# Gathered down rows of block 0 at the head of the scheduler's list in a hybrid mLSTM, attention and PEER layer

## The chip, the cores and the metric

The kernel runs on one core of a Trainium2 chip. The metric is the device time of one execution in microseconds (us): 3559.62 us before the change, the median of 3 runs (3559.3 to 3559.77). Lower is better. The engines are called PE (TensorE, matrix products), DVE (VectorE), ACT (ScalarE), POOL (GpSimd, which here only issues gathers) and SP (SyncE, which issues all other transfers).

## What is computed

One decoder layer on 1024 tokens of width 1024, in float32. The part that matters here, cut from the reference:

```python
proj = rmsnorm(x) @ w_in                     # queries, keys, values, gates
att_b = sliding_window_attention(...) @ w_branch_attn
ml_b = (mlstm_chunkwise(...) normed, gated) @ w_branch_mlstm
x = x + (sigmoid(gate_a) * att_b + sigmoid(gate_m) * ml_b) @ w_out
xb = rmsnorm(x)                              # PEER, per block of 128 tokens:
q = xb @ w_query
s = q against 2 x 128 sub keys, 8 heads      # scores
idx, gate = top 16 of the 16 x 16 sums of the two top 16, softmax
u = expert_down[idx]                         # 8 x 16 rows of 16384 for each token
act = gelu(sum over d of xb * u)
x = x + sum over k of gate * act * expert_up[idx]
```

## The kernel before, in words

The 1024 tokens are 8 blocks of 128. The **front** (`front`, L304) does the mixers, the residual and the PEER queries and scores for four groups of two blocks, one group after the other: groups 0 to 3 are blocks (0, 1), (2, 3), (4, 5) and (6, 7). Its weights come from HBM in tiles of 0.5 MB (`wpart`, L207), four of which are in flight (WB = 4); where the products are split for precision, ACT makes the high part `whi` (L214) and DVE the residual `wlo` (L215), and PE multiplies three times (L231 to L233). A weight tile serves 4 chunks of the contraction, for two blocks.

Within a group the order is: query, key and value projections, and the mLSTM's gate projections (`wif`); attention; the mLSTM; the gates with the branch projections (L229 on `attT` and `hmT`); the next group's normed input (`normed`); the output projection (L612, on `mixT`) with the addition of the residual (L614, `x2`); the query projection of PEER (L627, on `xbT`); and the scores (L640), which go to HBM and come back by block (L667, `sc<-sc_d`).

`topk` (L647, on DVE) finds the experts of a block. It is emitted for the group before, ahead of a group's front, with its priority put behind by LATER (`later`, L856), so that it fills gaps. For blocks 1 to 5, which are treated **densely**, `spread` (L712) writes the gates into a dense token by expert matrix: DVE makes one-hot operands `oi` and `oj` (L727, L730), PE multiplies them (L735), ACT copies (L736), SP stores (L738). The front calls it piece by piece (`fill`, L871) among the gates, the output and the query projection. Blocks 0, 6 and 7 are **sparse**: their expert rows are gathered.

After the front comes the dense part (`dense`): all experts in turn against blocks 1 to 5, PE bound, with the gathers and products of the sparse blocks spread through it, except one: block 0's rows of `expert_down`. These are gathered and multiplied in the front (`down`, L747, called at L884): 128 gathers on POOL (L743, `g<-down,idx`, 128 rows of 4 KB each) and 128 **products** on DVE (L756, a multiplication with `xb` summed over the row, which also reads out its accumulator into `act`). The pool `gather` (L98) has two tiles `g`; a gather waits until the product two before it has released its tile. The gathers need block 0's `idx`, which exists about 500 us into the run.

Each product is tied to an anchor: `pace` takes 128 evenly spaced ones of the marked matmuls of the front, from 0.4 to 0.95 of them, and `after` (L151) adds an order without a semaphore: the scheduler may place product i only after its anchor has been placed. Where it is placed from then on is up to priority: the scheduler builds each engine's list by taking, of the instructions that are ready in its own time, the one with the highest priority, and priority falls with the place in the program. `down` stands behind the whole front there. On the chip each engine then runs its list in order, and waits on semaphores only for data and buffers.

Of the kernel before, what the change touches and what calls it, by code (L numbers as in the profile page):

```python
# [88 lines left out]
def build(nc, tc, a, out, dbg=None):  # L89
# [8 lines left out]
    gp = pool("gather", 2)  # L98
# [52 lines left out]
    def after(ins, name):  # L151
        if name is not None:
            tc.add_manual_dep(ins.ins, name, NOSYNC, reason="pace")
# [587 lines left out]
    def fetch(p, table, idx, s):  # L741
        t = p.tile([P, D], F32, name="g")
        G.indirect_dma_start(out=t, out_offset=None, in_=a[table],  # L743
                             in_offset=bass.IndirectOffsetOnAxis(ap=idx[:, s:s + 1], axis=0))
        return t

    def down(r, b, pace, p):  # L747
        act = bp.tile([P, P], F32, name="act", bufs=1)
        xb = bp.tile([P, D], F32, name="xb", bufs=1)
        SY.dma_start(xb, xb_d[b])  # L750
        gain = p.tile([P, D], F32, name="g")
        SY.dma_start(gain, a["gain2"].to_broadcast([P, D]))
        V.tensor_tensor(xb, xb, gain, ALU.mult)
        for s in range(P):
            t = fetch(p, "down", r["idx"], s)
            ins = V.tensor_tensor_reduce(out=t, in0=t, in1=xb, scale=1.0, scalar=0.0, op0=ALU.mult,  # L756
                                         op1=ALU.add, accum_out=act[:, s:s + 1])
            after(ins, next(pace, None))
        coef = bp.tile([P, P], F32, name="coef")
        A.activation(coef, act, AF.Gelu)  # L760
        V.tensor_tensor(coef, coef, r["gate"].rearrange("p h k -> p (h k)"), ALU.mult)
        r["coef"] = coef
# [101 lines left out]
    res = {}  # L864
# [16 lines left out]
    names = anchors["front"]  # L881
    names = names[int(PACE0 * len(names)):int(PACE1 * len(names))]
    pace = iter([names[i * len(names) // P] for i in range(P)])
    down(res[0], 0, pace, gp)  # L884
    inner.close()
    gd = dense()
    names = anchors["dense"]
    pace = iter([names[int((PD0 + i * (PD1 - PD0) / (5 * P)) * len(names))] for i in range(5 * P)])
# [18 lines left out]
```

## Time and profile before

| | us |
|---|---|
| median of 3 runs | 3559.62 |
| the profiled execution, its time | 3545.12 |
| its span, first to last instruction | 3543.4 |
| PE busy | 3378.6 |
| DVE busy | 2743.1 |
| ACT busy | 1363.0 |
| POOL busy | 985.7 |

The profile is one execution on the chip. The front fills about the first half of the span, the dense part the rest. Busy shares are means over both. The views used below are: the page; the busy time of each engine in a window of the span; groups of instructions by line; waits, each put down to what ended it last; the chain of waits, which follows the work that ended last back in time; and the timeline. Times in them count from the start of the span.

### The profile page before, as it was taken

The numbers are of one execution on the slowest core, as the hardware profiler recorded it, in microseconds if no ns is written. First come the engines' busy times: TensorE is split into PE (matmuls) and PEld (weight loads), VectorE is DVE, ScalarE is ACT, GpSimd is POOL, SyncE is SP. The second block draws the span as 40 slices with busy tenths as digits, with TensorE's granted clock in tenths as the row PEclk, the third lists the DMA queues.
The fourth block names the chain that finished last, engine by engine and source line by source line (L and its number), as shares of the span: only waits on it lengthen the run. The fifth ranks groups of instructions, "written<-read, shape, count | busy, mean of one in ns | idle before, by whom it ended". The sixth has DMA issues, their size and how long they took to land.

```text
span 3543.4 us, 55473 instructions
## 1 busy us (share of the span) xinstructions
PE 3378.6 (95%) x20579; PEld 3044.3 (86%) x20579; DVE 2743.1 (77%) x6406; ACT 1363.0 (38%) x2730; POOL 985.7 (28%) x772
## 2 busy tenths in 40 slices
PE   7999999999998789989799999999999999999999
PEld 7898988888887678887688898999989999898998
DVE  5332689739898468988598988888888888889985
ACT  6652567338574346635322222222222222222221
POOL 0000000110001221110004654545455455545542
PEclk9999999999999888999899999999999999999999
DMA  4344434874378874686727988889888888888884
GB/s 149 108 143 166 164 115 145 256 261 141 117 212 252 274 247 150 206 244 174 252 101 276 329 307 321 321 284 329 285 315 305 294 321 299 312 308 302 325 288 160
DMA packets 386670, 846.66 MB, mean 239 GB/s; under 512 B 189280, under 2 KB 195168, under 8 KB 382304
## 3 DMA queue, kind: packets, MB, share of 16 engines
q1 hardware_dynamic: 275808, 440.42, 37.7%
q0 software_dynamic: 110592, 402.70, 32.5%
q8 instruction: 162, 2.65, 0.3%
q14 instruction: 108, 0.88, 0.1%
HBM read 780.11 MB, written 62.91 MB: 238 GB/s over the span
## 4 chain that ended last, share of the span: by engine, by line
PE 66%; DVE 13%; issue 8%; DMA 7%; POOL 3%; ACT 3%; SPq 0%; POOLq 0%; DVEq 0%; ACTq 0%
PE ph L809 19%; PE pj L229 8%; PE po L830 6%; PE po L833 6%; PE po L834 6%; PE pj L231 4%; PE pj L233 4%; PE pj L232 4%; DMA g<-down,idx 3%; POOL g L743 3%; DVE oi L727 2%; PE at L735 2%; DMA w<-wmain 1%; DVE g L756 1%; DMA g<-up,idx 1%
## 5 line engine op out<-in xcount | busy, mean ns | idle before, releaser
L743 POOL DMA_INDIRECT g<-down,idx x384 | 480.2, 1250 | 1769.3 <-DVE act L756 879.2
L743 POOL DMA_INDIRECT g<-up,idx x384 | 505.3, 1316 | 732.8 <-DVE acc L770 373.9
L756 DVE CUSTOM_DVE_ANT_0 g<-g,xb 128x1024 f32<-128x1024 f32 x384 | 462.6, 1219 | 167.2 <-DMA g<-down,idx 166.6
L770 DVE SCALAR_TENSOR_TENSOR acc<-g,coef,acc 128x1024 f32<-128x1024 f32 x384 | 491.7, 1281 | 46.8 <-DMA g<-up,idx 36.8
L830 PE MATMUL po<-hu,ah 128*128 128x512 f32 x1280 | 499.2, 390 | 2.3 <-DVE y L836 2.3
L809 PE MATMUL ph<-xbh,hd 128*128 128x320 f32 x2048 | 470.6, 311 | 31.7 <-ACT hd L797 22.8
L833 PE MATMUL po<-lu,ah 128*128 128x512 f32 x1280 | 498.5, 389 | 0.0
L834 PE MATMUL po<-hu,al 128*128 128x512 f32 x1280 | 498.1, 389 | 0.0
L809 PE MATMUL ph<-xbh,ld 128*128 128x320 f32 x2048 | 470.5, 311 | 5.3 <-DVE ld L798 5.3
L809 PE MATMUL ph<-xbl,hd 128*128 128x320 f32 x2048 | 469.9, 311 | 0.0
L797 ACT CAST hu<-rawu 128x1024 fp32r<-128x1024 f32 x128 | 131.5, 1051 | 738.9 <-PE po L834 557.0
L809 PEld LDWEIGHTS ph<-xbh,hd 128*128 128x128 f32 x2048 | 346.6, 189 | 35.3 <-ACT hd L797 23.2
L215 DVE TENSOR_TENSOR wlo<-w,whi 128x1024 fp32r<-128x1024 f32 x200 | 243.3, 1218 | 142.1 <-ACT whi L214 142.0
L809 PEld LDWEIGHTS ph<-xbh,ld 128*128 128x128 f32 x2048 | 345.1, 189 | 7.0 <-DVE ld L798 6.7
L809 PEld LDWEIGHTS ph<-xbl,hd 128*128 128x128 f32 x2048 | 345.6, 189 | 0.0
L214 ACT CAST whi<-w 128x1024 fp32r<-128x1024 f32 x200 | 209.3, 1047 | 235.9 <-DMA w<-wmain 100.1
L836 DVE TENSOR_TENSOR y<-po,y 128x512 f32<-128x512 f32 x320 | 218.2, 685 | 89.0 <-PE po L834 88.5
L830 PEld LDWEIGHTS po<-hu,ah 128*128 128x128 f32 x1280 | 240.3, 188 | 53.9 <-DVE y L836 4.7
L834 PEld LDWEIGHTS po<-hu,al 128*128 128x128 f32 x1280 | 240.3, 188 | 50.5 <-DVE al L820 0.3
L833 PEld LDWEIGHTS po<-lu,ah 128*128 128x128 f32 x1280 | 240.3, 188 | 48.5
L232 PE MATMUL pj<-wlo,hT 128*128 128x256 f32 x832 | 244.9, 295 | 23.9 <-DVE wlo L215 23.9
L231 PE MATMUL pj<-whi,hT 128*128 128x256 f32 x832 | 245.9, 296 | 1.1 <-ACT whi L214 1.1
(266 smaller groups left out, 6670.2 us busy)
## 6 DMA issues: line engine op xcount, KB each, us to landing
w<-wmain SPq DMA_DIRECT2D x328, 512.0 KB
rawd<-downT SPq DMA_DIRECT2D x128, 512.0 KB
rawu<-up SPq DMA_DIRECT2D x128, 512.0 KB
gate_d<-stage SPq DMA_DIRECT2D x40, 1024.0 KB
g<-gate_d SPq DMA_DIRECT2D x32, 1280.0 KB
x<-x SPq DMA_DIRECT2D x16, 512.0 KB
sc_d<-sc SPq DMA_DIRECT2D x16, 512.0 KB
sc<-sc_d SPq DMA_DIRECT2D x32, 256.0 KB
```

The costliest lines, as they stand in the source:

```text
L215: V.tensor_tensor(lo, t, hi.bitcast(F32), ALU.subtract)
L229: ins = T.matmul(ps, lh(c), rh(c), start=first, stop=last)
L231: T.matmul(ps, lh(c), rh(c), start=first, stop=False)
L232: T.matmul(ps, lh(c), rl(c), start=False, stop=False)
L743: G.indirect_dma_start(out=t, out_offset=None, in_=a[table], in_offset=bass.IndirectOffsetOnAxis(ap=idx[:, s:s + 1], axis=0))
L756: ins = V.tensor_tensor_reduce(out=t, in0=t, in1=xb, scale=1.0, scalar=0.0, op0=ALU.mult, op1=ALU.add, accum_out=act[:, s:s + 1])
L770: ins = V.scalar_tensor_tensor(acc, t, g, acc, ALU.mult, ALU.add)
L809: ins = T.matmul(ps[:, u, 0:W], w[:, c, :], x[:, c, u * W:u * W + W], start=first, stop=last)
L830: first = T.matmul(o, ah[:, tok], uh[:, cols], start=(e == 0), stop=False)
L833: T.matmul(o, ah[:, tok], ul[:, cols], start=False, stop=False)
L834: ins = T.matmul(o, al[:, tok], uh[:, cols], start=False, stop=(e == EG - 1))
L836: V.tensor_tensor(y[:, k, cols], o, y[:, k, cols], ALU.add)
```

## The change

The call of `down` for block 0 is put into the scheduler's `high_priority` block. Everything that it issues (the load of `xb`, the load of `gain2`, the product of both, the 128 gathers, the 128 products, the gelu and its gating) then has a higher priority than everything else. The anchors stay. The number and kind of instructions are the same.

```diff
--- before.py
+++ after.py
@@ -881,7 +881,8 @@
     names = anchors["front"]
     names = names[int(PACE0 * len(names)):int(PACE1 * len(names))]
     pace = iter([names[i * len(names) // P] for i in range(P)])
-    down(res[0], 0, pace, gp)
+    with tc.high_priority():
+        down(res[0], 0, pace, gp)
     inner.close()
     gd = dense()
     names = anchors["dense"]
```

What it moves, at three places. In the names the number behind the underscore is that of the tile; `g_17479` is the tile of product 1, and each further product's number is 3 higher.

On DVE, in the query and key projection of group 2 (`qkms` is the sum of squares of its heads, `sc`, `tv`, `ti`, `bps`, `bv` and `cand` belong to the top-k of block 2). Before:

```order
L215 TENSOR_TENSOR wlo_8860<-w_8857,whi_8859 128x1024
L318 TENSOR_REDUCE qkms_7939<-sq_8262 128x2
L655 MAX_INDEX bps_7500<-bv_7471,cand_7497 128x8
L657 MATCH_REPLACE cand_7497<-bv_7471,cand_7497 128x136 x2
L659 MAX bv_7471<-cand_7497 128x8
L318 TENSOR_REDUCE qkms_7939<-sq_8267 128x2
```

And now:

```order
L215 TENSOR_TENSOR wlo_8860<-w_8857,whi_8859 128x1024
L756 ISA g_17569,act_17473<-g_17569,xb_17474 128x1024
L756 ISA act_17473 128x1
L318 TENSOR_REDUCE qkms_7939<-sq_8262 128x2
L659 MAX tv_7473<-sc_7475 128x8
L661 MAX_INDEX ti_7474<-tv_7473,sc_7475 128x8
L215 TENSOR_TENSOR wlo_8894<-w_8891,whi_8893 128x1024
L756 ISA g_17572,act_17473<-g_17572,xb_17474 128x1024
L756 ISA act_17473 128x1
L318 TENSOR_REDUCE qkms_7939<-sq_8267 128x2
```

Products 31 and 32 now stand here, and the top-k, which had got to its candidates, is at its first maxima still.

On DVE, behind group 2's last addition of `x2`, where the first three weight residuals of group 3 (`wlo_12751` and two more) stand. Before, the end of a row of 14 products, of which `g_17701` is product 75:

```order
L756 ISA g_17698,act_17473<-g_17698,xb_17474 128x1024
L756 ISA act_17473 128x1
L756 ISA g_17701,act_17473<-g_17701,xb_17474 128x1024
L756 ISA act_17473 128x1
L215 TENSOR_TENSOR wlo_12751<-w_12748,whi_12750 128x1024
L756 ISA g_17704,act_17473<-g_17704,xb_17474 128x1024
L756 ISA act_17473 128x1
L215 TENSOR_TENSOR wlo_12781<-w_12778,whi_12780 128x1024
L756 ISA g_17707,act_17473<-g_17707,xb_17474 128x1024
L756 ISA act_17473 128x1
L215 TENSOR_TENSOR wlo_12811<-w_12808,whi_12810 128x1024
```

And now, the end of a row of 5 products, with `g_17722` product 82:

```order
L756 ISA g_17716,act_17473<-g_17716,xb_17474 128x1024
L756 ISA act_17473 128x1
L756 ISA g_17719,act_17473<-g_17719,xb_17474 128x1024
L756 ISA act_17473 128x1
L756 ISA g_17722,act_17473<-g_17722,xb_17474 128x1024
L756 ISA act_17473 128x1
L215 TENSOR_TENSOR wlo_12751<-w_12748,whi_12750 128x1024
L215 TENSOR_TENSOR wlo_12781<-w_12778,whi_12780 128x1024
L215 TENSOR_TENSOR wlo_12811<-w_12808,whi_12810 128x1024
L756 ISA g_17725,act_17473<-g_17725,xb_17474 128x1024
```

Five products are left ahead of the three residuals and none between them; the others of that row stand in group 2 now.

On PE, at the end of group 2's gates (`hmT`) and the start of its output projection (`mixT`); L735 are the spread's products, of block 3, L716 and L269 transposes. Before:

```order
L229 MATMUL pj<-hmT,w 128x256 x4
L735 MATMUL at<-oj,oi 128x128 x4
L229 MATMUL pj<-hmT,w 128x256 x4
L735 MATMUL at<-oj,oi 128x128 x4
L229 MATMUL pj<-hmT,w 128x256 x4
L735 MATMUL at<-oj,oi 128x128 x4
L229 MATMUL pj<-hmT,w 128x256 x8
```

And now:

```order
L229 MATMUL pj<-hmT,w 128x256 x32
L229 MATMUL pj<-w,mixT 128x256 x16
L716 MATMUL tp<-identr,ef 128x128
L269 MATMUL tp<-identr,scr 128x128 x4
L229 MATMUL pj<-w,mixT 128x256 x4
L716 MATMUL tp<-identr,ef 128x128
L716 MATMUL tp<-identr,dgate 128x128
L229 MATMUL pj<-w,mixT 128x256 x2
L269 MATMUL tp<-identr,scr 128x128 x4
L229 MATMUL pj<-w,mixT 128x256
L735 MATMUL at<-oj,oi 128x128 x3
```

The spread's products of block 3 have left the gates, and begin in the output projection, behind the transposes of block 3's experts (L716).

## Rows read from the trace of the kernel before

**Rows 1.** Page, part 1: busy us (share of the span) and instructions of each engine.

```profile
PE 3378.6 (95%) x20579; PEld 3044.3 (86%) x20579; DVE 2743.1 (77%) x6406; ACT 1363.0 (38%) x2730; POOL 985.7 (28%) x772
```

**Rows 2.** Windows: busy us (instructions) of each engine, granted clock, DMA share, GB/s.

```profile
336.00:410.00 74.00, 71.75 (x482) 67.28 (x480) 26.15 (x70) 29.38 (x57) 0.00 (x0) 0.94 0.60 201
742.00:815.00 73.00, 70.52 (x483) 65.68 (x482) 35.08 (x90) 29.05 (x56) 8.26 (x8) 0.97 0.80 271
797.00:947.00 150.00, 149.26 (x1114) 128.97 (x1112) 138.49 (x555) 100.51 (x255) 4.31 (x3) 0.93 0.41 142
947.00:1191.00 244.00, 220.91 (x1411) 200.28 (x1410) 208.11 (x769) 136.00 (x332) 30.62 (x31) 0.95 0.76 222
1191.00:1299.00 108.00, 79.80 (x483) 73.27 (x481) 51.18 (x85) 30.49 (x57) 32.23 (x27) 0.83 0.81 274
...
1540.00:1600.00 60.00, 51.33 (x299) 45.82 (x299) 48.56 (x159) 14.46 (x31) 11.14 (x10) 0.94 0.84 266
```

**Rows 3.** Chain of waits, 1191 to 1299 us: shares of that stretch by line.

```profile
by line: issue 61.8%; POOL g L743 21.9%; DMA g<-down,idx 6.5%; PE pj L232 3.7%; PE pj L233 3.4%; PE pj L231 3.1%; DVE wlo L215 1.0%; POOLq L743 0.3%; DVE ti L655 0.3%; DVE tv L653 0.3%; DVE g L756 0.2%; DVE act L756 0.1%; DVEq L756 0.0%
```

**Rows 4.** Timeline of DVE: start us, us, what; in brackets idle before and releaser.

```profile
1199.47 1.23 DVE L756 CUSTOM_DVE_ANT_0 g<-g,xb 128x1024 f32<-128x1024 f32 x1 [5.78 <-DMA g<-down,idx]
...
1207.45 1.23 DVE L756 CUSTOM_DVE_ANT_0 g<-g,xb 128x1024 f32<-128x1024 f32 x1 [5.17 <-DMA g<-down,idx]
```

**Rows 5.** Windows for L756 alone: DVE busy us (records, two for a product).

```profile
742.00:815.00 73.00, 9.84 (x16) 0.97 0.80 271
797.00:947.00 150.00, 3.12 (x6) 0.93 0.41 142
947.00:1191.00 244.00, 38.00 (x62) 0.95 0.76 222
1191.00:1299.00 108.00, 33.24 (x54) 0.83 0.81 274
```

**Rows 6.** Waits of PE, 1191 to 1299 us: us in total, times, longest us.

```profile
PE pj L232 <- DVE wlo L215: 23.0, 4, 10.5
```

**Rows 7.** Chain of waits, 620 to 700 us: start us, us, what.

```profile
651.21 8.77 DMA g<-down,idx
...
664.10 0.12 PE pj L231
```

**Rows 8.** Page, part 5: busy us, mean ns of one, then idle before.

```profile
L756 DVE CUSTOM_DVE_ANT_0 g<-g,xb 128x1024 f32<-128x1024 f32 x384 | 462.6, 1219 | 167.2 <-DMA g<-down,idx 166.6
```

**Rows 9.** Waits of DVE, 947 to 1191 us.

```profile
DVE g L756 <- DMA g<-down,idx: 24.2, 13, 4.6
```

**Rows 10.** Waits of PE, 947 to 1191 us.

```profile
PE at L735 <- DVE oj L730: 12.8, 7, 4.2
PE at L735 <- DVE oi L727: 5.0, 1, 5.0
```

**Rows 11.** Groups by line, PE, 742 to 815 us: busy us, mean ns, idle before.

```profile
L229 PE MATMUL pj<-xbT,w 128*128 128x256 f32 x128 | 28.4, 385 | 0.0
```

**Rows 12.** Chain of waits, 1500 to 1700 us.

```profile
1548.54 7.24 issue
1556.01 7.78 DMA g<-down,idx
```

**Rows 13.** Groups by line, 960 to 1010 us.

```profile
L727 DVE TENSOR_SCALAR oi<-iota,cols 128x128 f32<-128x128 f32 x47 | 14.8, 338 | 0.3 <-ACT cols L717 0.3
...
L730 DVE TENSOR_SCALAR oj<-iota,cols 128x128 f32<-128x128 f32 x34 | 9.3, 277 | 0.0
```

**Rows 14.** Groups by line, 1066 to 1180 us.

```profile
L727 DVE TENSOR_SCALAR oi<-iota,cols 128x128 f32<-128x128 f32 x118 | 37.9, 355 | 2.0 <-PE at L735 2.0
...
L730 DVE TENSOR_SCALAR oj<-iota,cols 128x128 f32<-128x128 f32 x87 | 24.9, 286 | 0.0
...
L743 POOL DMA_INDIRECT g<-down,idx x24 | 23.2, 966 | 94.9 <-DVE act L756 50.9 <-DVE oi L727 43.0 <-DVE hTlow L277 1.1
```

**Rows 15.** Waits of SyncE's DMA queue, 797 to 947 us.

```profile
SPq L667 <- DVE ti L661: 16.5, 3, 15.5
```

## Prediction

> **What bounds the kernel now.** I read the page's busy shares first [rows 1]: TensorE (PE) is busy for 95% of the span, so work taken off another engine pays only where PE waits for it. The next view is therefore the busy time by stage [rows 2]. One stage comes back after each group of the front: from the query projection (L627) of one group, over its scores, to the end of the query, key and gate projections of the next. It is the same PE work each time, 482 or 483 matmul records, yet it took 74 us after group 0, 73 us after group 1 and 108 us after group 2. PE was busy in these for 71.75, 70.52 and 79.80 us, so the third has 28 us in which PE stood still; and its granted clock, which has the two levels 2.4 and 1.2 GHz, averaged 0.83 where the others had 0.94 and 0.97, so PE also spent more time on the same matmuls.
>
> What it waited for is in the chain of waits of that stage [rows 3]: "issue" 61.8%, the issue of gathers on GpSimd (POOL) 21.9%, gathers landing 6.5%, and hardly any PE. VectorE's (DVE) timeline shows why [rows 4]: one product of block 0 (L756) after another, with 5.78 and 5.17 us idle until a gather landed. The gather pool has two tiles, so a gather starts when the product two before it is done, and a run of products goes at the pace of gathers: 27 products (54 records, two each) in 108 us, 4 us each [rows 5]. In VectorE's order the weight residuals (wlo, L215) of group 3 stand behind 14 such products in a row, and PE waits 23.0 us for wlo in this stage [rows 6]. The same stage held 8 products after group 1 [rows 5] and none after group 0. So this stage is bound by a run of gathers, not by PE.
>
> The stretch before it (797 to 1191 us, group 2 itself) is another matter: VectorE was busy there for 138.49 of 150 and 208.11 of 244 us [rows 2], with 3 and 31 products [rows 5]. Most of the products due in the first of these windows came in the second or in the lump behind it, after top-k and spread work that stood ahead of them.
>
> **The change, part by part.** No instruction is added or taken away; block 0's gathers, products, gain load and gain product only move. The order shows where: of the 128 products, 1 to 3 come forward a little, 4 to 28 stay where they were, 29 to 76 come forward from the lump into group 2, most of the rest stay within some thirty places, and 115 to 121 come forward in group 3. GpSimd's order is the same list of gathers. SyncE's differs in where score reloads and spread stores stand among weight loads; the gain load goes to the front of its list, which costs one 0.5 MB transfer at the start and nothing on the path. From about 1680 us of before on, the orders of PE, VectorE and ScalarE are the same again, so the dense part shifts as a whole. I sum against the profiled execution (3545.12 us, span 3543.4); the median of the timed runs, 3559.62, is 14.5 us above it, and I carry the sum over unchanged.
>
> A. Around 650 us. In before, product 3 waited for a gather that could start only after product 1, which stood behind a block of spread work: 8.77 us of the chain [rows 7]. Products 1 and 2 now stand ahead of most of that spread work, so gather 3 has landed by the time product 3 is due. They also push 2 x 1.22 us [rows 8] into a stretch full of spread work. Between 8.77 - 2.44 = 6 us saved and 2 us lost; I take 4 saved, nearer the first, since the wait was on the chain.
>
> B. 797 us to the last addition of group 2's x2 (L614). By the order, 48 products stand ahead of that addition where 31 did: 17 more, 17 x 1.22 = 20.7 us of VectorE time, in a stretch that VectorE already bounds. What goes is its waiting for gathers, 24.2 us [rows 9]: 48 products over the 394 us of the two windows have 8 us each, twice the pace of 4 us. The difference is 3.5 us saved. But the spread work now comes in one bunch late in the group, with little PE work left to mix with; the price if PE and VectorE hand it to each other one by one is bounded by what PE lost to spread operands here, 12.8 + 5.0 = 18 us [rows 10]. I take 0, between 6 saved (every wait gone and two products' time hidden) and 18 lost, nearer to the difference, since both engines have the same work in sum.
>
> C. The 108 us stage. Now 5 products instead of 14 stand in a row ahead of group 3's first wlo: 5 x 4 = 20 us of gather pace, started when the x2 addition is done, against 28.4 us of query projection on PE [rows 11]; they are hidden. About 13 products fall in the stage, between the 8 of group 1 (73 us) and the 27 of before (108 us). On a line between these it would be 73 + 5 x 35/19 = 82 us; but at 4 us each 13 products need 52 us, less than PE's 73, so I take 75: 33 saved. The bounds are the 73 of group 1 and the 82 of the line, 35 and 26 saved. Part of this is clock: the matmuls that took 79.80 us of PE time here took 70.52 us after group 1.
>
> D. Group 3. Products 115 to 121 leave the lump at 1540 us, where the chain shows 7.24 us of issue and 7.78 us of a gather landing [rows 12] and PE was busy for 51.33 of 60 us [rows 2]. At most the 8.7 us of PE's gap and a little clock, 12 saved; at worst those 7 products delay spread work that PE waits for by 7 x 1.22 = 8.5 us, less the gap they leave, 5 lost. I take 5 saved: VectorE does the same work before the group's end either way.
>
> Sum: -4 + 0 - 33 - 5 = -42 us, 3503 in the profiled execution's terms, **3518 us** in the runs'. All good ends together are -6 - 6 - 35 - 12 = -59, all bad ends together +2 + 18 - 26 + 5 = -1.
>
> One thing speaks against moving gathers among spread work. The rows: the spread operands took 338 and 277 ns (oi, oj) in a stretch with one gather [rows 13] and 355 and 286 ns in one with 24 [rows 14]; 118 x 17 + 87 x 9 ns = 2.8 us, or 0.12 us per gather, 2 us for the 17 gathers that now fall there, inside B's bounds. The Trainium skill (SBUF — State Buffer, section Who interferes with whom) has VectorE and GpSimd share a port pair that the first to start holds for its whole instruction, and names tensor_scalar, which the spread operands are, among those that can take it. By that rule each of the 17 gathers could hold VectorE for its whole issue, and the sum would be some 16 us poorer; the trace's 0.12 us says that it hardly does.
>
> **The rivals.** (1) B goes wrong by its bound: spread products, bunched behind the moved products, hand PE and VectorE their operands one by one. For it: the bunch stands in the order; against it: x2's output projection is now mixed into it matmul by matmul. -42 + 18 = -24, 3536 us. (2) Each gather holds VectorE for its issue, 0.97 us [rows 14], 17 times in the bound stretch: -42 + 16 = -26, 3534 us. The row of 0.12 us speaks against it. (3) Nothing to be measured: the gather waits only move. Where pairs of products stand closer than 8 us the wait comes back, all 24.2 us of B's saving is lost (+18 by B's own bound), C gives its poorer 26, and A and D come out at +2 and 0: -6, 3554 us. For it: a few pairs in the order stand close together; against it: gathers landed in time wherever products were 8 us apart. (4) Slower: weight loads behind score reloads on SyncE. Top-k gives way to the products, so its score tiles come free later, and a reload (L667) at the head of SyncE's queue holds back the weights behind it. The longest such wait in before was 15.5 us [rows 15], most of which the weight tiles ahead of PE covered: four of them, each good for 24 matmuls (4 chunks, 2 blocks, 3 products) of 0.12 us [rows 7], 11.5 us. If all 16 reloads of groups 2 and 3 waited so long, PE would lose 16 x 4 = 64 us: -42 + 64 = +22, 3582 us; it is slower from the eleventh such wait on, and measurably so from the thirteenth. Against it: the reloads now stand further apart among the weights. (5) That the change does nothing can be ruled out by the order.
>
> **How the numbers follow.** The forecast, 3518, has a chance of 0.61; its own bounds are 3503 to 3538. Rival 1 has 0.18, rival 2 0.05, rival 3 0.09, rival 4 0.07. A measurement of this kernel tells about 0.2%, 7 us, from no change: below 3552.5 is faster. Forecast and rivals 1 and 2 make faster 0.84; rival 3 gives same 0.09, rival 4 slower 0.07. The range runs from 3503 to 3553: it leaves out rival 4, most of rival 3 and a little below C's and D's good ends, less than 2 in 10.
>
> **What would show it.** In the profile after: the stage from group 2's query projection to group 3's projections at some 75 us with a granted clock above 0.9 and PE's wait for wlo a few us (C); VectorE's waits for gathers ahead of it near zero, and group 2's query projection starting at 1185 to 1190 us (A, B); no lump at the end of group 3 (D). If that projection starts after 1200 us, or if PE waits for spread operands by more than 18 us there, B failed; if gathers still fill the chain of the stage, C did; if weight loads wait for score reloads and PE for weights, rival 4 is the case. The dense part must keep its length; a change there would be outside this reasoning.

## The result and the profile after

| | before | after |
|---|---|---|
| median of the timed runs, us | 3559.46 (4 runs, 3551.92 to 3559.77) | 3510.82 (4 runs, 3506.36 to 3514.14) |
| ratio | | 0.9868, 95% interval 0.985 to 0.9885 |
| the profiled execution's span, us | 3543.4 | 3509.5 |
| PE's granted clock over the span | 0.966 | 0.969 |

The change makes the kernel 48.6 us faster by the medians (interval 41 to 53, from the ratio, which is estimated from all runs); 3518 us were forecast, with a range of 3503 to 3553. The two profiles are only 33.9 us apart. Where the other 15 us come from is taken up below.

The page after, PE's total and the products, answers to [rows 1] and [rows 8]:

```profile
PE 3384.0 (96%) x20579; PEld 3042.5 (87%) x20579; DVE 2741.8 (78%) x6406; ACT 1368.1 (39%) x2733; POOL 983.2 (28%) x772
...
L756 DVE CUSTOM_DVE_ANT_0 g<-g,xb 128x1024 f32<-128x1024 f32 x384 | 462.7, 1219 | 81.0 <-DMA g<-down,idx 80.5
```

PE's busy time is what it was, so what has gone is PE standing still: 3543.4 - 3378.6 = 164.8 us before, 3509.5 - 3384.0 = 125.5 us now. VectorE stands still 81.0 us ahead of products, where it was 167.2. Both count the products of all three sparse blocks; 41 us of each lie in the dense part (from 1640 us on), so for block 0 in the front the wait fell from 125 to 40 us.

Windows of the kernel after: the first half of group 2, its second half, the stage from its query projection to group 3's projections, and the end of group 3. They answer to [rows 2], and the second fence, products alone, to [rows 5]:

```profile
820.00:955.00 135.00, 131.56 (x931) 110.93 (x931) 117.86 (x423) 87.40 (x220) 19.92 (x16) 0.89 0.49 163
955.00:1199.00 244.00, 231.27 (x1438) 203.69 (x1437) 231.47 (x894) 143.84 (x357) 31.00 (x30) 0.97 0.79 228
1199.00:1270.00 71.00, 68.14 (x478) 63.14 (x476) 33.61 (x66) 27.98 (x51) 14.21 (x12) 1.00 0.89 306
1505.00:1565.00 60.00, 59.00 (x400) 55.09 (x399) 58.69 (x196) 24.02 (x55) 8.36 (x8) 1.00 0.94 279
```

```profile
820.00:955.00 135.00, 19.59 (x32) 0.89 0.49 163
955.00:1199.00 244.00, 38.22 (x63) 0.97 0.79 228
1199.00:1270.00 71.00, 13.19 (x22) 1.00 0.89 306
```

The stage (1199 to 1270 us) takes 71 us where it took 108. It holds 11 products (22 records) where it held 27, PE is busy for 68.14 of 71 us at a granted clock of 1.00, the upper of its two levels. Group 2 ahead of it holds 47 products (95 records) in 379 us, where it was 33. The same 379 us of before:

```profile
812.00:1191.00 379.00, 355.17 (x2395) 314.25 (x2394) 332.14 (x1270) 228.94 (x571) 33.25 (x33) 0.94 0.62 187
```

VectorE is busy there for 117.86 + 231.47 = 349 us, where it was 332: 17 us more work in the same length.

The chain of waits of that stage, by line, answers to [rows 3], and PE's waits in it to [rows 6]:

```profile
by line: DMA w<-wmain 37.8%; PE pj L229 20.6%; PE pj L231 9.6%; PE pj L232 9.3%; PE pj L233 9.2%; ACT whi L214 4.4%; ACT sc L643 2.1%; DVE wlo L215 1.7%; SPq L644 1.7%; PE at L735 1.6%; ACT sq L317 0.7%; ACT qk L320 0.7%; issue 0.7%; SPq L2
```

```profile
PE pj L232 <- DVE wlo L215: 0.4, 1, 0.4
```

The gathers' issue on GpSimd and their landing, 22 and 7 per cent before, are gone from the chain. Of the 62 per cent of "issue" (time that the chain puts down to no wait; before, its pieces of up to 6 us lay between one gather's issue and the next) 0.7 are left. It now follows weight transfers (`w<-wmain`) and PE's own matmuls, and PE waits 0.4 us for residuals instead of 23.0.

VectorE's waits for gathers in the second half of group 2, and PE's for spread operands there, answer to [rows 9] and [rows 10]:

```profile
DVE g L756 <- DMA g<-down,idx: 3.7, 3, 1.4
```

```profile
PE at L735 <- DVE oj L730: 3.0, 6, 1.0
...
PE at L735 <- DVE oi L727: 0.4, 1, 0.4
```

24.2 us of waiting for gathers have become 3.7, and the spread products, bunched as the order said, do not make PE wait more: 3.0 + 0.4 us where it was 12.8 + 5.0.

**Where in the run the time went.** Five instructions serve as milestones in every kernel here: the last addition of `x2` (L614) of groups 0, 1, 2 and 3, and the last sum of squares (L318) of group 3's key projection, which ends the stage. The rows are VectorE's timeline grouped by line, with the first and last start of the group (us) before its shape. Before:

```profile
L614 DVE TENSOR_TENSOR x<-pj,x x4: 690/692/692, 310.7 to 326.2; 128x512 f32<-128x512 f32 x4
...
L614 DVE TENSOR_TENSOR x<-pj,x x4: 685/692/693, 716.5 to 732.0; 128x512 f32<-128x512 f32 x4
...
L614 DVE TENSOR_TENSOR x<-pj,x x4: 676/680/686, 1148.6 to 1179.4; 128x512 f32<-128x512 f32 x4
...
L318 DVE TENSOR_REDUCE qkms<-sq x6: 279/677/680, 1270.1 to 1297.7; 128x8 f32<-128x512 f32 x4, 128x2 f32<-128x128 f32 x2
...
L614 DVE TENSOR_TENSOR x<-pj,x x4: 671/682/691, 1651.9 to 1667.2; 128x512 f32<-128x512 f32 x4
```

After:

```profile
L614 DVE TENSOR_TENSOR x<-pj,x x4: 691/692/692, 318.7 to 334.2; 128x512 f32<-128x512 f32 x4
...
L614 DVE TENSOR_TENSOR x<-pj,x x4: 686/692/693, 723.4 to 739.0; 128x512 f32<-128x512 f32 x4
...
L614 DVE TENSOR_TENSOR x<-pj,x x4: 683/688/693, 1173.2 to 1187.5; 128x512 f32<-128x512 f32 x4
...
L318 DVE TENSOR_REDUCE qkms<-sq x6: 267/680/686, 1249.7 to 1268.7; 128x8 f32<-128x512 f32 x4, 128x2 f32<-128x128 f32 x2
...
L614 DVE TENSOR_TENSOR x<-pj,x x4: 692/696/702, 1617.3 to 1637.5; 128x512 f32<-128x512 f32 x4
```

The last starts of those rows give the first two lines of this table, and rows like them the others. A column is the length of a stretch; the number behind the kernel's name is its span. Column C begins at the last addition, some 11 us ahead of the query projection with which the windows of the stage begin.

| profile (span) | to group 0's end | group 1 | group 2 (B) | stage (C) | group 3 (D) | dense part |
|---|---|---|---|---|---|---|
| before (3543.4) | 326.2 | 405.8 | 447.4 | 118.3 | 369.5 | 1876.2 |
| after (3509.5) | 334.2 | 404.8 | 448.5 | 81.2 | 368.8 | 1872.0 |
| after, second profile (3504.9) | 326.5 | 408.0 | 451.8 | 82.2 | 364.9 | 1871.5 |
| gain load not moved (3503.8) | 330.6 | 405.3 | 450.4 | 79.6 | 362.5 | 1875.4 |
| products 29 to 84 (3503.7) | 330.7 | 410.3 | 448.9 | 81.5 | 354.8 | 1877.5 |
| all but 29 to 84 (3531.5) | 326.2 | 404.8 | 449.4 | 119.6 | 356.9 | 1874.6 |
| run held from 67 (3541.2) | 333.0 | 405.2 | 452.9 | 95.7 | 379.6 | 1874.8 |
| run held from 62 (3555.8) | 327.9 | 405.5 | 451.9 | 93.7 | 402.1 | 1874.7 |
| smaller pools (3566.7) | 326.4 | 411.3 | 456.2 | 114.5 | 365.2 | 1893.1 |
| smaller pools, three tiles (3540.5) | 326.5 | 411.1 | 449.5 | 90.4 | 371.8 | 1891.2 |
| anchors respaced (3534.9) | 332.9 | 414.4 | 452.9 | 100.0 | 359.4 | 1875.3 |
| three tiles, two of oi, oj (3516.1) | 332.8 | 406.7 | 455.1 | 81.7 | 368.7 | 1871.1 |
| three tiles, one of sc (3524.1) | 330.6 | 403.0 | 456.5 | 82.8 | 364.6 | 1886.6 |

The stage is where nearly all of the change is: 37 us. The dense part is 4 to 5 us shorter in both profiles of the change; no run here explains that. Group 0 is 8 us longer in the first profile after, though nothing but the gain load was moved there.

### The profile page after: what moved, and what is told of

Read it like the earlier page. It is cut to its first block, busy times and chain, and to the rows that moved or that the text cites. A ratio compares the mean times of both kernels' runs of the same rounds, so it can differ in the third digit from the quotient of the medians.

```text
span 3509.5 us, 55471 instructions
## 1 busy us (share of the span) xinstructions
PE 3384.0 (96%) x20579; PEld 3042.5 (87%) x20579; DVE 2741.8 (78%) x6406; ACT 1368.1 (39%) x2733; POOL 983.2 (28%) x772
## 4 chain that ended last, share of the span: by engine, by line
PE 68%; DVE 14%; DMA 7%; issue 6%; ACT 3%; POOL 2%; SPq 0%; POOLq 0%; DVEq 0%; ACTq 0%
PE ph L809 19%; PE pj L229 8%; PE po L834 7%; PE po L830 7%; PE po L833 7%; PE pj L233 4%; PE pj L231 4%; PE pj L232 4%; DVE oi L727 3%; POOL g L743 2%; DMA w<-wmain 2%; DVE oj L730 2%; DMA g<-down,idx 1%; DVE g L756 1%; DMA g<-up,idx 1%
## 5 line engine op out<-in xcount | busy, mean ns | idle before, releaser
L743 POOL DMA_INDIRECT g<-up,idx x384 | 501.7, 1307 | 736.6 <-DVE acc L770 379.6
L756 DVE CUSTOM_DVE_ANT_0 g<-g,xb 128x1024 f32<-128x1024 f32 x384 | 462.7, 1219 | 81.0 <-DMA g<-down,idx 80.5
```

What stands on the lines that cost most here:

```text
L743: G.indirect_dma_start(out=t, out_offset=None, in_=a[table], in_offset=bass.IndirectOffsetOnAxis(ap=idx[:, s:s + 1], axis=0))
```

## The experiments

Theory G: the gain is PE's no longer waiting, in the stage, for weight residuals that stand behind a run of products at the gathers' pace. Theory O: it comes from the other moves. The experiments also ask what the 8 us at the start are, and whether a better arrangement of the products is to be had. Behind a line that an edit adds, line numbers are one higher than before.

**1. The gain load left where it was.** Only the loop is at the highest priority:

```diff
-    with tc.high_priority():
-        down(res[0], 0, pace, gp)
+    down(res[0], 0, pace, gp)
...
         for s in range(P):
-            t = fetch(p, "down", r["idx"], s)
-            ins = V.tensor_tensor_reduce(out=t, in0=t, in1=xb, scale=1.0, scalar=0.0, op0=ALU.mult,
-                                         op1=ALU.add, accum_out=act[:, s:s + 1])
+            with tc.high_priority() if b == 0 and (True) else ExitStack():
+                t = fetch(p, "down", r["idx"], s)
+                ins = V.tensor_tensor_reduce(out=t, in0=t, in1=xb, scale=1.0, scalar=0.0, op0=ALU.mult,
+                                             op1=ALU.add, accum_out=act[:, s:s + 1])
             after(ins, next(pace, None))
```

> Like the changed kernel, but only the 128 gathers and products are at the highest priority; the load of the gain and its product stay at the end of the program's priorities. The lists of PE, VectorE, ScalarE and GpSimd are those of the changed kernel; on SyncE only the gain load (0.5 MB) is not at the front any more. Theory L (the gain load at the start delays the first weights, and with them everything, by the 8 us that the changed kernel was behind at 165 us): 8 us faster than the changed kernel, about 3503 us, with x's first stages back at the times of before. Theory C (the 8 us come from the clock's phases at the start, the load is nothing): 3508 to 3514 us, within 3 us of the changed kernel.

Measured: 0.9865 of before (0.9839 to 0.989; median 3506.55), which the intervals do not tell from the change's 0.9868. Its profile lost 4.4 us up to group 0's end, with the gain load late; so something other than the load costs those 4.4 us; experiment 9 comes back to it.

**2 and 3. One half of the products each.** The same edit with another condition:

```diff
-            with tc.high_priority() if b == 0 and (True) else ExitStack():
+            with tc.high_priority() if b == 0 and (28 <= s < 84) else ExitStack():
```

> Only products 29 to 84 and their gathers are at the highest priority, those that leave the run of 14 behind group 2 and stood in it. Theory G (the gain is PE's no longer waiting for weight residuals behind gather-paced products in the stage from group 2's query projection to group 3's projections): nearly the whole gain, 40 to 50 us faster than before, 3510 to 3520 us; that stage at about 75 us and PE's wait for residuals a few us. Theory O (the gain comes from the other moves, around 650 us and in group 3, or from the order of top-k and spread work): less than half of it, 3535 us or more.

and with `not 28 <= s < 84`:

> All products but 29 to 84 at the highest priority. Theory G: little, 0 to 10 us faster than before, 3550 to 3560 us, with the stage after group 2 still at 100 us or more. Theory O: more than half of the gain, 3535 us or less.

Measured: products 29 to 84 alone give 0.9859 (0.9829 to 0.989; median 3505.92), all of the change's gain. The others alone give 0.9956 (0.994 to 0.9972; median 3540.72), some 16 us by the ratio. The stage and PE's wait for residuals in it, first with 29 to 84, then with the others:

```profile
1200.00:1272.00 72.00, 69.07 (x484) 64.07 (x483) 35.01 (x69) 28.33 (x54) 14.24 (x12) 0.99 0.89 302
```

```profile
PE pj L232 <- DVE wlo L215: 0.3, 1, 0.3
```

```profile
1192.00:1301.00 109.00, 78.61 (x477) 72.64 (x476) 53.29 (x85) 29.93 (x55) 31.33 (x28) 0.81 0.81 277
```

```profile
PE pj L232 <- DVE wlo L215: 27.7, 5, 14.6
```

With products 29 to 84 moved, the stage is 72 us long and PE waits 0.3 us for residuals. With all others moved it is 109 us long, and PE waits 27.7 us at a mean granted clock of 0.81. Theory G has its main part. But the others were to give 10 us at most and gave more. By the table their gain is in group 3 (356.9 us for 369.5), where products 115 to 121 leave the lump. That the lump is the reason is not shown: with 29 to 84 alone the lump stays (PE is busy for 53.73 of the 59 us from 1508 to 1567), and group 3 is shorter still. The two gains, 50 and 16 us, add up to more than the whole, 49. Group 3 takes 354.8 and 356.9 us with either half moved, and 362.5 to 368.8 with both; why both together gain less there than each alone was not taken apart.

**4 and 7. The run held back.** Before, but product 67 (then 62) and the later ones are ordered behind the third residual of group 3:

```diff
+        first.append(len(anchors.get("wlo", [])))
         for s in range(3):
...
             after(ins, next(pace, None))
+            if b == 0 and s >= 66:
+                after(ins, anchors["wlo"][first[3] + 2])
```

where the residuals' names are noted in `anchors["wlo"]`, and 66 is 61 in the second.

> The kernel before, in which products 67 to 128 are moreover tied to the third weight residual of group 3 (an order, no semaphore), so that three residuals go ahead of the rest of the run; products still leave group 2 late. Theory G: this alone gives most of it, 20 to 33 us faster than before, 3527 to 3540 us, the stage after group 2 at 75 to 85 us, since the gather-paced run then lies beside PE's work; the rest is paid in group 3, which gets up to 10 more products. Theory O: no more than 8 us. A third possibility, that fewer products in the stage (DMA traffic beside the weights) is what matters and not their place: also no more than 8 us, with PE waiting for weights rather than residuals.

> As the kernel of the run that held back product 67 and the later ones, but from product 62 on: none of the run stands between group 2's last addition and the third residual of group 3. Theory G: PE's wait for residuals falls further, from 7.4 us to below 4, and the stage from 85 to 75 to 82 us; what is saved there is paid again in group 3, which gets five more products (5 x 1.22 us), so 3530 to 3540 us in all, within 8 us of that run. If instead the number of products in the stage counts, not their place, the stage gets longer than 85 us.

Measured: from 67 on 0.995 (0.9935 to 0.9966; median 3540.35), just under 18 us faster and a little less than expected; from 62 on 1.0016 (1.0004 to 1.0029; median 3558.15), no gain at all. The stage and PE's wait in it, held from 67, and the wait when held from 62:

```profile
1203.00:1288.00 85.00, 74.60 (x481) 69.67 (x480) 37.97 (x63) 29.66 (x55) 19.54 (x16) 0.91 0.82 279
```

```profile
PE pj L232 <- DVE wlo L215: 7.4, 2, 5.5
```

```profile
PE pj L232 <- DVE wlo L215: 9.3, 2, 6.5
```

Up to product 67 every engine's list is that of before. With three residuals set ahead of the run, the stage falls from 108 to 85 us. VectorE's timeline there shows what remains:

```profile
1223.58 1.23 DVE L757 CUSTOM_DVE_ANT_0 g<-g,xb 128x1024 f32<-128x1024 f32 x1 [6.79 <-DMA g<-down,idx]
...
1233.97 1.23 DVE L215 TENSOR_TENSOR wlo<-w,whi 128x1024 fp32r<-128x1024 f32 x1 [9.16 <-ACT whi L214]
...
1251.90 1.23 DVE L757 CUSTOM_DVE_ANT_0 g<-g,xb 128x1024 f32<-128x1024 f32 x1 [4.66 <-DMA g<-down,idx]
...
1254.45 1.23 DVE L757 CUSTOM_DVE_ANT_0 g<-g,xb 128x1024 f32<-128x1024 f32 x1 [1.31 <-DMA g<-down,idx]
...
1255.60 1.22 DVE L215 TENSOR_TENSOR wlo<-w,whi 128x1024 fp32r<-128x1024 f32 x1
```

The first residual at 1233.97 us waited for its weight (`whi`, on ScalarE) and no longer for products. The fifth, at 1255.60 us, stands behind two products, the first of which waited 4.66 us for its gather: the longer of PE's two waits, 5.5 of the 7.4 us, is for this residual. Held from 62 on, the wait is no smaller (9.3 us), since the same pairs of products then stand between the later residuals; that expectation was wrong, and so was that of 3530 to 3540 us in all. The stage held from 62 on, products alone:

```profile
1197.00:1280.00 83.00, 13.45 (x22) 0.92 0.77 254
```

It holds 11 products, as many as in the changed kernel, and takes 83 us instead of 71, at a lower DMA share (0.77, there 0.89). So it is the products' place that counts, and not their number or the traffic of their gathers.

What is held back comes due in group 3: 11 products more than before make it 10 us longer, 16 more make it 33 us longer. The step from 10 to 33 is more than five products' time; some of it is PE's wait for residuals again (14.9 us there, 4.9 when held from 67), and the rest stays open. So holding the run back shows the cause, but it is no remedy: the run is a debt from group 2, and has to be worked off where VectorE has time.

**5 and 6. The pace of the run.** A third gather tile needs room, so the control has the smaller pools alone:

```diff
-                    oi = ks.tile([P, 2, P], F32, name="oi", bufs=3)
-                    oj = ks.tile([P, 2, P], F32, name="oj", bufs=3)
+                    oi = ks.tile([P, 2, P], F32, name="oi", bufs=2)
+                    oj = ks.tile([P, 2, P], F32, name="oj", bufs=2)
...
-            sc = kp.tile([P, 4, P], F32, name="sc")
+            sc = kp.tile([P, 4, P], F32, name="sc", bufs=1)
```

> The kernel before with three pools made smaller to make room for the next run: two tiles each of oi and oj where there were three, one tile of sc where there were two. It is the control of the next run. Products still leave group 2 late (35 stand ahead of its last part, 80 ahead of group 3's third residual, as in before 33 and 76). Both theories: 3555 to 3580 us, no faster than before, the stage after group 2 at 105 us or more.

```diff
-    gp = pool("gather", 2)
+    gp = pool("gather", 3)
```

> The control with three gather tiles where there were two; nearly the same order on every engine. Theory G (the run of products goes at the pace of the gathers' round trip, two in flight, and PE waits behind it): three in flight make a product every 2.7 to 3.3 us instead of 4 to 5, the stage after group 2 shrinks by 20 to 35 us, and the kernel is 15 to 33 us faster than the control. If the traffic of gathers and weights sets the pace of the run (DMA share 0.81 in that stage), three in flight come no faster: within 5 us of the control. Theory O: within 5 us too.

Measured: the control 1.0068 (1.0048 to 1.0088; median 3575.74), with three tiles 0.9957 (0.994 to 0.9973; median 3537.92): 38 us from one more tile, more than the 15 to 33 expected (the two profiles are 26 us apart). The run of products in each (count, shortest/median/longest ns, first to last start), and PE's wait for residuals in the stage, control first:

```profile
L756 DVE CUSTOM_DVE_ANT_0 g<-g,xb x15: 1207/1225/1250, 1196.1 to 1252.3; 128x1024 f32<-128x1024 f32 x15
```

```profile
PE pj L232 <- DVE wlo L215: 20.4, 5, 11.4
```

```profile
L756 DVE CUSTOM_DVE_ANT_0 g<-g,xb x14: 1218/1224/1226, 1196.1 to 1233.2; 128x1024 f32<-128x1024 f32 x14
```

```profile
PE pj L232 <- DVE wlo L215: 1.5, 2, 0.9
```

With two tiles a product comes every (1252.3 - 1196.1) / 14 = 4.0 us, with three every (1233.2 - 1196.1) / 13 = 2.85 us; PE's wait falls from 20.4 to 1.5 us and the stage from 114.5 to 90.4. It is the round trip of a gather, divided by the tiles, that PE waited for, as theory G has it, and not the traffic.

**8. Anchors by VectorE's free time.**

```diff
-    names = names[int(PACE0 * len(names)):int(PACE1 * len(names))]
-    pace = iter([names[i * len(names) // P] for i in range(P)])
+    at = [m0 + (m1 - m0) * (i - p0) / (p1 - p0) for (p0, m0), (p1, m1) in zip(STEPS, STEPS[1:]) for i in range(p0, p1)]
+    pace = iter([names[int(m * len(names))] for m in at])
```

with STEPS = (0, 0.40), (14, 0.45), (40, 0.545), (74, 0.74), (92, 0.79), (122, 0.925), (128, 0.985), the loop as in experiment 1.

> All gathers and products at the highest priority, and their anchors spaced by VectorE's free time: from 0.40 of the anchors to 0.545, where VectorE was busy for half of the time, 40 products (33 in the changed kernel); to 0.74, where it was busy for 28 of each 30 us, 34; to 0.79, the stage after group 2, 18; to 0.925 30; and 6 to 0.985, where it stood still. If products cost their own time where VectorE bounds (about 0.9 us of 1.22 each), some 7 fewer in group 2 and 10 fewer in group 3's bound part make it 5 to 15 us faster than the changed kernel, 3492 to 3505 us. If gathers at 4.5 us apart are late, PE waits again for residuals and nothing is won: 3505 to 3520 us. Slower than that if the last products hold up the change from the front's pools to the dense part's.

Measured: 0.9935 (0.9915 to 0.9956; median 3531.71), some 25 us behind the change, so it was a loss. Group 1, which got more products, took 9 us longer than in experiment 1; group 2, which got 8 fewer, took 2.5 us more, not less; and the stage, with 15 products instead of 12, took 20 us more (waits for residuals 6.4 us, clock 0.92). Fewer products in group 2 buy nothing: VectorE's time is not what sets its length.

**9. The changed kernel again.** No edit.

> The changed kernel once more, with a second profile. The first pair of profiles had it 8 us behind before already at 165 us, where both run the same lists but for the gain load, and it lost 8 us more behind 1298 us that the kernel with the same lists but for the gain load's place did not lose. If that is the phase of the granted clock: 0.985 to 0.989 of before, as first measured, and in the new profile the lag at 165 us and the step behind 1298 us differ from the first by some us. If the gain load does it, the lag at 165 us is 8 us again.

Measured: 0.9863 (0.9844 to 0.9882; median 3507.27). Its profile has no lag at group 0's end (326.5 us, before 326.2), with the gain load at the front of the list. PE's windows near the start (the last three columns are granted clock, DMA share, GB/s): before, the first profile after, the second, and the run held from 67, whose gain load is late:

```profile
60.00:80.00 20.00, 19.64 (x150) 18.50 (x150) 16.79 (x56) 11.61 (x30) 0.00 (x0) 0.91 0.27 95
...
160.00:180.00 20.00, 20.00 (x169) 20.00 (x168) 7.71 (x7) 9.62 (x10) 0.00 (x0) 1.00 0.58 197
```

```profile
60.00:80.00 20.00, 19.64 (x130) 19.14 (x130) 12.70 (x33) 9.02 (x16) 0.00 (x0) 0.76 0.22 77
...
160.00:180.00 20.00, 20.00 (x134) 17.95 (x131) 6.64 (x13) 6.48 (x7) 0.00 (x0) 0.78 0.23 76
```

```profile
60.00:80.00 20.00, 19.63 (x150) 18.49 (x150) 16.59 (x55) 11.59 (x28) 0.00 (x0) 0.91 0.28 92
...
160.00:180.00 20.00, 20.00 (x169) 20.00 (x168) 7.48 (x7) 9.62 (x10) 0.00 (x0) 1.00 0.57 192
```

```profile
60.00:80.00 20.00, 19.64 (x135) 19.14 (x136) 13.84 (x43) 8.60 (x16) 0.00 (x0) 0.79 0.23 79
...
160.00:180.00 20.00, 20.00 (x140) 18.48 (x137) 6.67 (x11) 6.91 (x8) 0.00 (x0) 0.82 0.28 94
```

Where the lag is, the granted clock between 60 and 80 us is 0.76 or 0.79 and between 160 and 180 us 0.78 or 0.82; where it is not, 0.91 and 1.00. It comes with the gain load at the front and without (the held run has the lists of before there, and is 6.8 us behind it), and stays away with it at the front. So it goes with the clock that one execution was granted, and not with the change; why the clock was lower in these executions is not shown.

**10 and 11. The change with three gather tiles.** The edit of experiment 1 and three gather tiles, with one tile of `ef` and of the dense gates; then two tiles of `oi` and `oj` in the one, one tile of `sc` in the other.

> All gathers and products at the highest priority, as in the kernel that differs from the changed one by the gain load alone, with three gather tiles; room is made by two tiles each of oi and oj for three, and one of ef and of dense gates for two. Theory G: no run of products stands ahead of PE's residuals any more, so a third tile has little left to give: VectorE's waits for gathers, 81 us in the changed kernel over the whole front, fall below 30 us, but they lie beside PE's work; 0 to 8 us from the third tile. The smaller pools cost something in the spread's work, at most the 22 us of the control with fewer oi, oj and sc tiles. So 3500 to 3525 us. If gathers still bound the front, 20 us or more faster than the changed kernel, below 3492 us.

> The same with three tiles of oi and oj as before, and one tile of sc instead of two. Theory G as above, 0 to 8 us from the third tile; which of the two smaller pools made the control slow tells itself apart here: if it was sc, this is the slower of the two, 3515 to 3530 us, and the other 3500 to 3510 us; if oi and oj, the other way round.

Measured: 0.9879 (0.986 to 0.9897; median 3514.24) and 0.989 (0.9871 to 0.9909; median 3519.63), neither better than the change. The page of the first, the products' row:

```profile
L757 DVE CUSTOM_DVE_ANT_0 g<-g,xb 128x1024 f32<-128x1024 f32 x384 | 462.8, 1220 | 52.2 <-DMA g<-down,idx 51.5
```

That row counts the products of all three sparse blocks, and so do the 81 us that the expectation names. In the front alone (400 to 1640 us), first the changed kernel, then three tiles:

```profile
DVE g L756 <- DMA g<-down,idx: 39.6, 18, 5.9
```

```profile
DVE g L757 <- DMA g<-down,idx: 9.0, 4, 3.3
```

VectorE's wait for gathers did fall there, to 9.0 us, below the 30 expected, and the kernel is no faster for it: with the run gone, gathers no longer set a length. What the smaller pools cost beside it is not known, as no run has them with two gather tiles and the moved products, so a gain of a few us from the third tile could be hidden. The one with a single `sc` tile is the slower, as expected if `sc` was the culprit, but the intervals overlap, and the other was to reach 3500 to 3510 us. By the table it loses in the dense part's first stretch (1886.6 us, like the control's 1893.1), the other in group 2 and 3. No run here beats the change by more than its interval; products 29 to 84 alone do as well.

## Why the prediction was right, point by point

**The bound.** That the stage was bound by a run of gathers and not by PE is shown from three sides: taking the run out (experiment 2), setting residuals ahead of it (4), and making it quicker in place (6) each shorten the stage, and moving everything else (3) does not.

**A**, forecast -4: group 1 changes by -1.0 and +2.2 us in the two profiles after, -0.5 with the gain load late. It is zero within what executions differ by, and reaches just past the bad end of the bounds (-6 and +2). Product 3's wait left the chain, but the stretch did not get shorter by it. The 8.77 us of the chain were the wrong measure: PE's own wait behind that product (for `wlo`, L233, 630 to 735 us) was 2.9 us, of which 0.3 are left, and waits for weights of 0.9 and 2.4 us, which before did not have there, have come up in the two profiles after.

**B**, forecast 0 (6 saved to 18 lost): +1 to +4 us in the four profiles in which the 17 products moved into group 2. The trade that it was made of happened: 17 us more of VectorE's work in the same 379 us, paid from its waits for gathers. But that VectorE bounds the stretch, as the forecast had it, is not borne out: 17 products more cost 1 to 4 us and 8 fewer (experiment 8) gained nothing. PE is busy for 363 of the 379 us there (355 before). The sign named for A and B, a query projection that starts at 1185 to 1190 us, did not come: it started at 1198.5 and 1197.3 us (before 1191.1), in the first profile by the 8 us of group 0, in the second by A and B themselves (+2.2 and +4.4). Rival 1, the bunched spread, did not come: PE waits 3.4 us for spread operands.

**C**, forecast -33 (-26 to -35): -36 to -39 us. Mechanism and place were right, and the term was a little small, past its good end. That end was the stage of group 1, 73 us at a clock of 0.97 with 8 products [rows 2, 5]. With 11 to 12 products it took 71 to 72 us at 0.97 to 1.00, so PE's own time was the right measure and the line between 8 and 27 products the wrong one: the length is PE's until a residual is late, and experiment 8, at 15 products, is on the other side. The 37 us are 25 of PE standing still (28.2 before, 2.9 after) and 12 of PE's busy time (79.80 to 68.14) for the same work at the higher clock.

**D**, forecast -5 (-12 to +5): -0.7 and -4.6 us after, -7.0 in experiment 1. The first of these holds a stretch from 1270 to 1392 us at a granted clock of 0.83, against 0.88 and 0.90 for the same stretch in the other two. PE's gap at the lump closed as forecast: it is busy for 59.00 of 60 us there (1505 to 1565 us), where it was 51.33 [rows 2]. But the gap does not decide the group's length. Group 3 as a whole, before, after and with products 29 to 84 alone:

```profile
1299.00:1668.00 369.00, 352.27 (x2327) 305.95 (x2327) 333.43 (x1269) 208.35 (x523) 44.14 (x39) 0.95 0.64 189
```

```profile
1270.00:1638.00 368.00, 357.51 (x2351) 312.32 (x2352) 332.87 (x1263) 213.71 (x529) 42.74 (x37) 0.94 0.64 189
```

```profile
1272.00:1627.00 355.00, 341.22 (x2327) 302.57 (x2327) 327.83 (x1244) 213.23 (x525) 43.21 (x37) 0.95 0.64 193
```

PE stands still for 10.5 us after, where it was 16.7, but is busy 5 us longer; and the third, which keeps the lump, is the shortest, by PE's busy time. What sets that stays open.

**The dense part** is 4.2 and 4.7 us shorter in the two profiles after, and 0.8 in experiment 1, which is outside the reasoning of the forecast and not explained. The gain load cost nothing (experiments 1 and 9), as said.

**The transfer from profile to runs** is the loosest step: the sum, -42 us against the profiled execution, was carried to the median unchanged. Profiles give -34 to -40 us, runs -49. So it is in part luck that 3518 lies so near 3510.82: A to D come to -38 and -34 us in the two profiles of the change and not to -42, C having given more than forecast and A, B and D together less, and the runs gained another 10 to 15 us that no term held. The 51 runs of before that were taken beside the experiments lie between 3542.66 and 3573.97 us, with mean granted clocks from 0.966 (the four fastest at 0.965 or 0.966) down to 0.961 (the slowest); the profiled execution, 3545.12 at 0.966, is one of its fastest. The 8 runs of the changed kernel lie between 3505.24 and 3514.14, at 0.969 to 0.973. So part of the gain in the runs is that before more often ran at a lower mean clock. Against the median of those 51 runs (3554.86), the 8 runs of the changed kernel (3509.1) are 46 us faster. That the waits in the stage do it is likely, since the clock there was 0.83, but was not shown by itself.

**The other rivals.** Rival 2, a gather that holds VectorE for its whole issue: between 1066 and 1187 us, with 15 gathers, the spread operands took (mean ns after the busy time)

```profile
L727 DVE TENSOR_SCALAR oi<-iota,cols 128x128 f32<-128x128 f32 x132 | 42.9, 343 | 0.0
...
L730 DVE TENSOR_SCALAR oj<-iota,cols 128x128 f32<-128x128 f32 x98 | 27.5, 280 | 0.0
...
L743 POOL DMA_INDIRECT g<-down,idx x15 | 15.9, 1057 | 72.4 <-DVE act L756 32.4 <-DVE oi L727 14.4 <-DVE oj L730 11.1
```

against 338 and 277 ns with one gather [rows 13]: 132 x 5 + 98 x 3 ns = 1 us, or 0.06 us per gather. The Trainium skill (SBUF — State Buffer, section Who interferes with whom) has VectorE, in its modes that use two ports, contend with GpSimd for a shared port pair, held by whoever issues first for a whole instruction, with the other fully blocked. By that rule the delay could fall on either engine. VectorE shows next to none; the gather's issue, though, took 1057 ns here against 966 in before [rows 14], so what there is of it may fall on GpSimd, where it costs nothing. Rival 3 needed the waits to come back, and in group 2 3.7 us did. Rival 4, weights behind score reloads, did not come: the longest wait of a reload rose from 15.5 to 19.9 us (739 to 1640 us), but PE waits for weights for only 0.6 us in that stretch, where it was 3.4.

## What to carry to other kernels

A side stream that shares an engine with a critical one costs little while it is spread out, and its full round trip as soon as it falls due in a run: here products cost next to nothing where they stood 8 us apart, and 37 us where 14 of them stood ahead of one operand that PE needed and more between the next ones. So look for runs of the side stream in the order, directly ahead of what the critical engine waits for, and price them at round trip over buffers; a priority that keeps the stream on its pace cures it, and one more buffer eases it (the stage went from 118 to 81 us with the one, from 114 to 90 with the other). When a profile pair and the timed runs disagree, see where the profiled execution lies among its runs and at which clock.

## What the runs showed of the hardware

A gather of 512 KB, from the release of its tile to the end of the product that uses it, takes 2 x 4.0 = 8.0 us with two tiles and 3 x 2.85 = 8.6 us with three, while weights stream beside it at a DMA share of 0.8 to 0.96; of that the product is 1.22 us and the issue about 1. The Trainium skill (DMA: Bandwidth & Descriptors, section Anatomy of one DMA — SWDGE (gpsimd) path) gives 2.0 us and the bytes at 436 GB/s; an estimate by it is 2.0 + 1.2 = 3.2 us for such a transfer, and 5.4 with issue and product, less than the 8 measured here, so here the measured pace is the one to use. No run shows whether the traffic beside it or the many rows of a gather make the difference.

One kernel varies by almost 1% from execution to execution (before: 3542.66 to 3573.97 us) with the granted clock: with the same lists of instructions the way to group 0's end took 326.5 us in one profile of the changed kernel and 334.2 in another.
